# The low half of a split state on VectorE in two pieces, the first gather taken apart among the up products, and the expert ids written first

## The chip, the core and the metric

The kernel runs on one NeuronCore of a Trainium2 chip. TensorE (PE in the rows, PEld for its weight loads), VectorE (DVE), ScalarE (ACT) and GpSimd (POOL) compute; SyncE (SP) issues the DMAs that bring the weights from HBM. The metric is the device time of one execution in microseconds. Three runs of the kernel before gave a median of 1363.94 us.

## What is computed

Two transformer blocks stand behind each other; the second has two layers. Each of the three layers ends in a mixture of experts over 256 tokens of width 1024: 32 experts in 4 groups, of which every token takes two. Cut to the part that the change touches:

```python
logit_g = (h @ w_rg + b_rg).astype(F32)
grp = jnp.argmax(logit_g, axis=-1)
logit_e = (h @ w_re + b_re).astype(F32).reshape(n_tok, N_GROUPS, EXPERTS_PER_GROUP)
logit_e = jnp.take_along_axis(logit_e, grp[:, None, None], axis=1)[:, 0]
top_v, top_i = lax.top_k(logit_e, TOP_K)
gate = jax.nn.softmax(top_v, axis=-1) * p_grp
...
def expert_block(args):
    xb, e = args
    g, u = jnp.split(xb @ w_up[e], 2, axis=-1)
    return (jax.nn.silu(g) * u) @ w_down[e]
```

The state `h` is the RMS-normed residual stream. The second block's layers do the same with a hidden width of 256 where the first has 512. All data is float32.

## The kernel before

**Stages.** `first_phase` computes the first block's attention and `second_phase` that of a layer of the second block. Each ends in `out_route`, which projects the attention's output, adds it to the residual X, and routes the tokens. `moe_phase` then runs the experts. So there are three boundaries between an attention and its experts, at about 280, 815 and 1147 us of the trace. In the rows they are told apart by these times.

**Weights.** All weights go through one `Stream`: a list of 1 MB pieces in a fixed order, and a ring of 23 SBUF slots. `pump` issues pieces on SP's queue as long as slots are free; `release` gives a slot back and pumps. SP works its queue strictly in order: an issue whose slot is still read by somebody holds up all that stand behind it. It also waits until the DMA eight places before it has landed, so at most eight are in flight. The experts of a layer come in blocks `p`. The first two blocks are static: their experts are known when the program is built, and their 24 pieces can be issued before the routing is done. From the third block on the experts are those that the routing ranks highest. Their pieces are in the stream as functions: `pump` stops at them until `publish` has filed the routing under its key, and then SP loads each expert's number from the tile `info` (lines 429 and 446) before it issues.

**The router in two token halves.** In `out_route` a token half `a` has 128 tokens. `choose(a)` is a chain of 18 small VectorE operations (lines 689 to 706) that ends in the mask `mk`. `place(a)` counts with TensorE (lines 715 and 717) each token's place in its expert, and VectorE writes `rpm` (line 718). `split(a)` takes the normed state apart into a high half `xh` (ScalarE, line 721) and a low half `xl`, the rounding rest, which the float32r matmuls need both of. For `a == 0` VectorE computes `xl` in one operation over 1024 columns (line 723). For `a == 1` ScalarE writes the normed state into a spare tile (line 726) and GpSimd subtracts (line 727). After it the slots `spent[1]` and `X.u` are released, in that order.

**The first experts.** In `moe_phase`, `sel_p(0)` builds the selection matrix P from `rpm` (line 1488). `gather(0, dp)` for dp = 0 to 3 fills two of the eight column blocks of `xg` each: 8 matmuls `xh`, `xl` by P into one PSUM bank (line 1520), one copy out by ScalarE (line 1528) and one by VectorE (line 1530 or 1532). `up(p)` multiplies `xg` with the up weights, column block by column block `dt` = 0 to 7 (line 1704); after every second `dt` in the first block's layer, after every fourth in the second block's, it releases the slots that it has used. For p = 0 it calls `hooks` between the column blocks: `rank_experts` (after dt 1), `place_units` and `gates` (after dt 3), `publish` (after dt 5), `unit_gates` (after dt 7). `publish` computes the ids (line 1614) and two further tables (lines 1617 to 1620) on TensorE, and then VectorE writes `info` (line 1621). `mm()` hands out PSUM banks in turn: two in the first block's layer, three in the second block's.

**Order.** The schedule is manual: each engine works its instructions in the order in which the program calls them. The tiles' readers and writers give the waits.

Of the kernel before, what the change touches and what calls it, by code (L numbers as in the profile page):

```python
# [10 lines left out]
F32 = mybir.dt.float32  # L11
F32R = mybir.dt.float32r
I32 = mybir.dt.int32
AF = mybir.ActivationFunctionType
# [358 lines left out]
def hybrid_kernel(ctx: ExitStack, tc: tile.TileContext, A, out, dbg=None):  # L373
# [115 lines left out]
    def cmc(n):  # L489
        return cm[:, CM[n][0]:CM[n][1]]  # L490
# [112 lines left out]
    def out_route(kind, O, E, finish, wr, brow, xT, tmp, spent):  # L603
# [31 lines left out]
        def group(a, c0, n, j):  # L635
            po = R.mm()[:, 0:n]
            sl = slice(c0, c0 + n)
            out_mm(O, po, a, sl, range(8))
            finished(po, a, sl, j)
# [29 lines left out]
        def scored(a):  # L669
            dve.scalar_tensor_tensor(R.L[:, a], pls[a][:, 0:36], rr[a], brow, op0=OP.mult, op1=OP.add)  # L670
# [39 lines left out]
        def place(a):  # L710
            mkf = R.mk.rearrange("p a g e -> p a (g e)")
            if a == 0:
                R.pr = R.mm()
            o = R.pr[:, 32 * a:32 * a + 32]
            pe.matmul(o, lhsT=cmc("strict"), rhs=mkf[:, a], start=True, stop=(a == 0), skip_group_check=True)
            if a == 1:
                pe.matmul(o, lhsT=ones, rhs=mkf[:, 0], start=False, stop=True, skip_group_check=True)
            dve.scalar_tensor_tensor(R.rpm[:, a], o, 1.0, mkf[:, a], op0=OP.add, op1=OP.mult)

        def split(a):  # L720
            act.activation(xh[:, a], X.t[:, a], AF.Copy, scale=rr[a])
            if a == 0:
                dve.scalar_tensor_tensor(xl[:, a], X.t[:, a], rr[a], xh[:, a].bitcast(F32), op0=OP.mult, op1=OP.subtract)
            else:
                t = tmp[:, 0:1024]
                act.activation(t, X.t[:, a], AF.Copy, scale=rr[a])
                pool.tensor_sub(xl[:, a], t, xh[:, a].bitcast(F32))

        group(0, 512, 512, 1)
        trans(0, 0, 4, True)  # L730
# [5 lines left out]
        scored(0)  # L736
        choose(0)
        split(0)
        group(1, 512, 256, 3)
        trans(1, 0, 4, False)  # L740
        group(1, 768, 256, 4)
# [5 lines left out]
        root(1)  # L747
        logits(1, range(4, 8))
        scored(1)
        choose(1)  # L750
        place(0)
        for j in range(4):
            start_y(j)
        place(1)
        split(1)
        S.release(*spent[1], X.u)
        R.xh, R.xl = xh, xl
        return R

# [682 lines left out]
    def moe_phase(kind, l, R, final=None):  # L1442
# [7 lines left out]
        with ExitStack() as es:  # L1450
# [81 lines left out]
                        dve.tensor_scalar(xg[:, dt], o, s, None, op0=OP.mult)  # L1532

            sel_p(0)
            cn = wx.tile([32, 1], F32, name="cn")
            dve.tensor_copy(cn, pr[0:32, 64:65])
            for dp in range(4):
                gather(0, dp)
            mark("moe")

            th = wx.tile([32, 4], F32, name="th")
# [70 lines left out]
            def publish():  # L1612
                pq = mm()
                pe.matmul(pq[0:1, 0:NS], lhsT=cmc("eid")[0:32], rhs=ind, start=True, stop=True)
                for a in range(2):
                    o = pq[:, 64 + a * NS:64 + (a + 1) * NS]
                    pe.matmul(o, lhsT=R.rT[:, a * 128:(a + 1) * 128], rhs=ind, start=True, stop=False,
                              skip_group_check=True)
                    pe.matmul(o[:, NR:], lhsT=ones[0:32], rhs=base, start=False, stop=True, skip_group_check=True)
                    pe.transpose(pq[0:32, 256 + a * 128:384 + a * 128], R.Gd[:, a], ident)  # L1620
                dve.tensor_copy(R.info[:, 0:NS], pq[0:1, 0:NS])
                R.rp = wx.tile([128, 2, NS], F32, name="rp")
                dve.tensor_copy(R.rp.rearrange("p a u -> p (a u)"), pq[:, 64:64 + 2 * NS])
                R.regs = {}
                routes[key] = R
                S.pump()
                R.gT = wk.tile([32, 256], F32, name="yl")
                act.activation(R.gT, pq[0:32, 256:512], AF.Copy)

# [15 lines left out]
            class Ring:  # L1645
# [21 lines left out]
                def up(self, p, dt, hf):  # L1667
                    if dt % per == 0 and hf == 0:
                        self.us = self.units(p, ("up", dt), blocks[p].n)
                    return [u.t.rearrange("p (k c) -> p k c", k=per)[:, dt % per, hf * 512:(hf + 1) * 512]  # L1670
                            for u in self.us]
# [34 lines left out]
            def up(p, src, hooks=()):  # L1706
                c = (p % 2) * 128
                pu = R.up()
                xg = grp[p // 2][2]
                hooks = dict(hooks)  # L1710
                for dt in range(8):
                    for hf in range(nh):
                        pair_mm(pu[:, hf * 512:(hf + 1) * 512], lambda a, b: xg[:, dt, c + a:c + b], src.up(p, dt, hf),
                                dt == 0, dt == 7)
                    src.up_done(p, dt)
                    for h in hooks.get(dt, ()):
                        h()
                hd = wk.tile([128, hid], F32, name="hd")
                act.activation(hd, pu[:, 0:hid], AF.Silu)  # L1719
                dve.tensor_mul(hd, hd, pu[:, hid:uw])  # L1720
                st[p] = K()
                st[p].hd = hd
# [100 lines left out]
                    act.preload_act_table_set("natural_log_exp_and_others")  # L1823
                    spare(p + 1, nun)

            count_hooks = {1: [rank_experts], 3: [place_units, gates], 5: [publish], 7: [unit_gates]}
            ring_src = Ring(S)
            ng = (NL + 1) // 2
            ALL = [(0, 0), (1, 0), (0, 1), (1, 1)]
            for p in range(NL + 1):  # L1830
                g = p // 2
                if p == NL - 2:
                    nun = nc.values_load(R.info[0:1, NS:NS + 1], engines=[ENG.PE, ENG.Activation, ENG.DVE, ENG.Pool],
                                         min_val=0, max_val=SPARE)
                if p == NL - 1:
                    S.reserve(5 if final == 1 else 6)
                if p == NL:
                    scat(p - 2, ALL[2:])
                    down(p - 1, ring_src)
                    break  # L1840
                if p > 0 and p % 2 == 0 and g + 1 < ng:
                    sel_p(g + 1)
                if p == 0:
                    up(p, ring_src, count_hooks)
                    sel_p(1)
                    sel_g(0)
                else:
                    up(p, ring_src)
                for z in range(2):
                    if p % 2 == 1 and g + 1 < ng:  # L1850
                        for dp in (2 * z, 2 * z + 1):
                            gather(g + 1, dp)
                    if p >= 2 and z == 0:
                        scat(p - 2, ALL[2:])
                if p % 2 == 1 and g + 1 < ng:
                    sel_g(g + 1)
                if p == NL - 1:
                    act.preload_act_table_set("natural_log_exp_and_others")
                    spare(NL, nun)
                if p > 0:  # L1860
                    down(p - 1, ring_src)
                tr(p)
# [428 lines left out]
```

## Time and profile before

| | |
|---|---|
| median of 3 runs (lowest to highest) | 1363.94 us (1363.77 to 1364.64) |
| the profiled execution: its own time, its span | 1363.06 us, 1361.4 us |
| busy share of the span: PE, PEld, DVE, ACT, POOL | 89%, 48%, 31%, 25%, 7% |
| weight queue: share of the 16 DMA engines, data | 82.2%, 458.04 MB |
| chain that ended last: PE, DMA, DVE, ACT | 54%, 33%, 6%, 4% |
| granted TensorE clock, mean | 0.96 |

The busy shares are averages over stages that differ: in some the PE sets the pace, in others the DMA queue has no gap. The chain of waits tells which, stretch by stretch. A granted clock of 1.00 is 2.4 GHz and 0.50 is 1.2 GHz. A row of a timeline gives start, duration, engine, line, operation and tiles, and in brackets the idle time before it.

### The profile page before, as it was taken

To read this page: it belongs to the slowest core of one execution; us is meant where nothing else is said; L and a number is where in the kernel's file an instruction comes from. 1 tells how busy PE (TensorE), PEld (TensorE's weight loads), DVE (VectorE), ACT (ScalarE), POOL (GpSimd) and SP (SyncE) were. 2 spreads that over 40 slices of the span, in tenths; PEclk is the share of its full clock that TensorE was granted. 3 is DMA by queue.
4 is the path that set the end of the run, shared out by engine and by line. 5 is a ranking of instruction groups with operands and counts; after the bars stand their busy time and mean duration, and the time that the engine had idled before them with its cause. 6 is when DMAs were issued, how large, how long until landed. Compare 5 with 4: busy or idle time off the path is not lost.

```text
span 1361.4 us, 18797 instructions
## 1 busy us (share of the span) xinstructions
PE 1205.6 (89%) x7310; PEld 652.9 (48%) x7310; DVE 424.1 (31%) x1001; ACT 338.6 (25%) x696; POOL 93.9 (7%) x79
## 2 busy tenths in 40 slices
PE   5999999999977799999679998998778999999775
PEld 3788765554221154443158655443217756444211
DVE  5456453352101021221155444221005535322102
ACT  4432343221000010110146522211015642212102
POOL 1344100000000000000012100000000210000000
PEclk9999999999988899999889999999889999999998
DMA  9645517959999999999994548999999365899995
GB/s 370 256 178 186 201 32 321 389 217 394 421 421 421 422 421 420 422 420 421 420 419 180 220 191 341 420 421 421 421 418 403 124 278 216 362 421 421 421 421 227
DMA packets 64540, 459.45 MB, mean 337 GB/s; under 512 B 7408, under 2 KB 7728, under 8 KB 9904
## 3 DMA queue, kind: packets, MB, share of 16 engines
q1 hardware_dynamic: 64432, 458.04, 82.2%
q8 instruction: 65, 1.06, 0.3%
q14 instruction: 43, 0.35, 0.1%
HBM read 466.40 MB, written 1.05 MB: 343 GB/s over the span
## 4 chain that ended last, share of the span: by engine, by line
PE 54%; DMA 33%; DVE 6%; ACT 4%; issue 2%; POOL 0%; SPq 0%; ACTq 0%; DVEq 0%; POOLq 0%
DMA ring<-in_dn_dram 14%; PE up L1704 12%; PE ps L561 10%; DMA ring<-in_gu_dram 10%; DMA ring<-in_up_dram 9%; PE mm L1704 6%; PE mm L596 5%; PE mm L1520 3%; PE ps L2001 3%; PE tr L596 2%; PE po L1770 1%; PE ps L957 1%; PE tr L1770 1%; PE ps L1972 1%; PE po L2125 1%
## 5 line engine op out<-in xcount | busy, mean ns | idle before, releaser
L1704 PE MATMUL up<-ring,xg 128*32 128x512 f32 (+2 forms) x2016 | 368.0, 632 | 55.1 <-DMA ring<-in_gu_dram 31.5
L1704 PEld LDWEIGHTS up<-ring,xg 128*32 128x32 f32 (+2 forms) x2016 | 103.9, 126 | 288.5 <-issue 184.8
L1704 PE MATMUL mm<-ring,hdT 128*32 128x512 f32 (+2 forms) x1008 | 192.7, 633 | 29.9 <-DMA ring<-in_dn_dram 18.3
L561 PE MATMUL ps<-ring,ring 128*128 128x256 f32 (+1 forms) x960 | 144.5, 308 | 1.4 <-POOL ring L896 0.6
L561 PEld LDWEIGHTS ps<-ring,ring 128*128 128x128 f32 x960 | 129.2, 192 | 20.9 <-issue 4.8
L1720 DVE TENSOR_TENSOR hd<-hd,up 128x256 f32<-128x256 f32 (+1 forms) x32 | 16.7, 520 | 358.0 <-ACT hd L1719 339.5
L1704 PEld LDWEIGHTS mm<-ring,hdT 128*32 128x32 f32 (+2 forms) x1008 | 52.4, 125 | 143.3 <-issue 97.9
L1719 ACT ACTIVATE hd<-up 128x256 f32<-128x256 f32 (+1 forms) x32 | 14.9, 465 | 369.3 <-PE up L1704 369.3
L1520 PEld LDWEIGHTS mm<-P,ring 128*128 128x128 f32 x512 | 66.6, 200 | 12.4 <-issue 9.0
L1520 PE MATMUL mm<-P,ring 128*128 128x256 f32 x512 | 70.6, 295 | 0.6 <-DVE xg L1530 0.3
L596 PE MATMUL mm<-ring,ring 128*128 128x512 f32 (+1 forms) x192 | 64.1, 487 | 0.0
L1746 DVE SCALAR_TENSOR_TENSOR yl<-mm,gt,yh 128x512 fp32r<-128x512 f32 x38 | 28.5, 751 | 110.3 <-ACT yh L1745 110.3
L1745 ACT ACTIVATE yh<-mm,gt 128x512 fp32r<-128x512 f32 x38 | 26.1, 687 | 105.2 <-PE mm L1704 70.2
L1741 DVE SCALAR_TENSOR_TENSOR mm<-mm,gt,gmod 128x512 f32<-128x512 f32 x24 | 18.2, 758 | 106.7 <-PE mm L1704 106.7
L1742 ACT ACTIVATE yh<-mm 128x512 fp32r<-128x512 f32 x23 | 13.7, 597 | 141.2 <-DVE mm L1741 141.2
L2001 PE MATMUL ps<-ring,ring 128*128 128x256 f32 x384 | 48.6, 286 | 0.0
L2001 PEld LDWEIGHTS ps<-ring,ring 128*128 128x128 f32 x384 | 46.9, 192 | 0.7 <-ACT ring L1977 0.4
L596 PEld LDWEIGHTS mm<-ring,ring 128*128 128x128 f32 x192 | 35.8, 190 | 23.7 <-issue 21.5
L1984 POOL TENSOR_SCALAR ring<-ring,fr 128x1024 f32<-128x1024 f32 x2 | 6.7, 3370 | 421.2 <-DMA ring<-in_win_dram 421.2
L822 POOL TENSOR_TENSOR ring<-ring,ring 128x1024 fp32r<-128x1024 f32 x12 | 29.9, 2492 | 58.0 <-ACT ring L821 50.9
L1954 DVE TENSOR_TENSOR ring<-ring,ring 128x1024 fp32r<-128x1024 f32 x24 | 29.0, 1255 | 13.3 <-ACT ring L1950 13.3
L1770 PE MATMUL po<-yh,sm 128*128 128x512 f32 x61 | 30.6, 502 | 1.7 <-ACT yh L1742 1.0
(460 smaller groups left out, 1336.9 us busy)
## 6 DMA issues: line engine op xcount, KB each, us to landing
ring<-in_gu_dram SPq DMA_DIRECT2D x128, 1024.0 KB, 19.7
ring<-in_dn_dram SPq DMA_DIRECT2D x124, 1024.0 KB, 19.7
ring<-in_up_dram SPq DMA_DIRECT2D x120, 1024.0 KB, 19.5
ring<-in_wmod_dram SPq DMA_DIRECT2D x24, 1024.0 KB, 6.9
ring<-in_win_dram SPq DMA_DIRECT2D x24, 1024.0 KB, 11.4
ring<-in_wout_dram SPq DMA_DIRECT2D x12, 1024.0 KB, 18.4
ring<-in_c_dram SPq DMA_DIRECT2D x2, 896.0 KB, 13.7
ring<-in_wsm_dram SPq DMA_DIRECT2D x2, 784.0 KB, 14.9
```

Source lines behind the costliest of these rows:

```text
L561: pe.matmul(out, lhsT=a, rhs=b, start=first and i == 0, stop=last and i == 2, skip_group_check=True)
L596: pe.matmul(po, lhsT=O.mixT[:, s, a * 128:(a + 1) * 128], rhs=O.w[2 * c + s // 4][:, s % 4, sl.start - 512 * c:sl.stop - 512 * c], start=( ...
L822: (pool if q else dve).tensor_sub(lo[:, sl], u.t[:, sl], hi[:, sl].bitcast(F32))
L1520: pe.matmul(o, lhsT=xx[:, a, dt * 128:(dt + 1) * 128], rhs=P[:, a], start=(k == 0), stop=(k == 3))
L1704: pe.matmul(out[w * e:w * e + w], lhsT=x_of(w * e, w * e + w), rhs=wt, start=start, stop=stop)
L1720: dve.tensor_mul(hd, hd, pu[:, hid:uw])
L1741: dve.scalar_tensor_tensor(pd, pd, s.gt, gmod[:, hf * 512:(hf + 1) * 512], op0=OP.mult, op1=OP.mult)
L1745: act.activation(yh, pd, AF.Copy, scale=s.gt)
L1746: dve.scalar_tensor_tensor(yl, pd, s.gt, yh.bitcast(F32), op0=OP.mult, op1=OP.subtract)
L1770: pe.matmul(y[2 * a + hf], lhsT=s.sm[:, a * 128:(a + 1) * 128], rhs=s.y[hf][i], start=False, stop=True, skip_group_check=True)
L1954: dve.tensor_sub(lo[:, sl], u.t[:, sl], hi[:, sl])
L2001: pe.matmul(p[:, f * 256:(f + 1) * 256], lhsT=w[pw][:, dt, f * 128:(f + 1) * 128], rhs=hT[ph][:, dt], start=(i == 0 and f == 0 and dt == 0 ...
```

## The change

It has four parts. The function names are those of the section above; line numbers in the rows of the changed program are some lines higher.

- `split(1)` loses its second ScalarE pass and the GpSimd subtraction and is called before `choose(1)`. VectorE computes `xl` of the second token half as it does for the first, by a new `split_low`, in two pieces of 512 columns: one between the two `place` calls, the other in `R.rest()`, which `moe_phase` calls after `sel_p(0)`.
- The release of `spent[1]` and `X.u` moves with the second piece into `R.rest()`.
- The four parts of the first gather become hooks. Parts 0 and 1 stand before the up products, with `rank_experts` between them. Parts 2 and 3 stand between the up products.
- `publish` computes the ids alone, files the routing and pumps. The two tables that it also made move into `tables`, called after `gates`. `place_units` and `publish` come earlier: after dt 0 and dt 1 in the first block's layer, after dt 1 and dt 3 in the second block's.

```diff
         def split(a):
             act.activation(xh[:, a], X.t[:, a], AF.Copy, scale=rr[a])
-            if a == 0:
-                dve.scalar_tensor_tensor(xl[:, a], X.t[:, a], rr[a], xh[:, a].bitcast(F32), op0=OP.mult, op1=OP.subtract)
-            else:
-                t = tmp[:, 0:1024]
-                act.activation(t, X.t[:, a], AF.Copy, scale=rr[a])
-                pool.tensor_sub(xl[:, a], t, xh[:, a].bitcast(F32))
+
+        def split_low(a, c0, c1):
+            dve.scalar_tensor_tensor(xl[:, a, c0:c1], X.t[:, a, c0:c1], rr[a], xh[:, a, c0:c1].bitcast(F32), op0=OP.mult,
+                                     op1=OP.subtract)
...
+        split(1)
         choose(1)
         place(0)
+        split_low(1, 0, 512)
         for j in range(4):
             start_y(j)
         place(1)
-        split(1)
-        S.release(*spent[1], X.u)
+
+        def rest():
+            split_low(1, 512, 1024)
+            S.release(*spent[1], X.u)
+        R.rest = rest
...
             sel_p(0)
+            R.rest()
             cn = wx.tile([32, 1], F32, name="cn")
             dve.tensor_copy(cn, pr[0:32, 64:65])
-            for dp in range(4):
-                gather(0, dp)
...
             def publish():
                 pq = mm()
                 pe.matmul(pq[0:1, 0:NS], lhsT=cmc("eid")[0:32], rhs=ind, start=True, stop=True)
+                dve.tensor_copy(R.info[:, 0:NS], pq[0:1, 0:NS])
+                R.regs = {}
+                routes[key] = R
+                S.pump()
+
+            def tables():
+                pq = mm()
                 for a in range(2):
...
-            count_hooks = {1: [rank_experts], 3: [place_units, gates], 5: [publish], 7: [unit_gates]}
+            first = [lambda dp=dp: gather(0, dp) for dp in range(4)]
+            if kind == 1:
+                first_hooks = {-1: [first[0], rank_experts, first[1]], 0: [place_units], 1: [publish, first[2]],
+                               3: [gates, first[3]], 5: [tables], 7: [unit_gates]}
+            else:
+                first_hooks = {-1: [first[0], rank_experts, first[1]], 1: [place_units], 3: [publish, first[2]],
+                               4: [gates, first[3]], 6: [tables], 7: [unit_gates]}
```

VectorE at the first boundary, before, from the last operation of `choose(1)` (`mk`) to the key of the ranking (`kd`); `xg` is the gathered state:

```order
L706 TENSOR_TENSOR mk<-o_2071,o_2072 128x32 [waits DVE_49]
L718 SCALAR_TENSOR_TENSOR rpm<-mm,mk 128x32 [waits PE_49]
L718 SCALAR_TENSOR_TENSOR rpm<-mm,mk 128x32 [waits DVE_49,PE_49]
L1460 COPY bias_2264<-modT 128x8
L1488 TENSOR_TENSOR P<-cm,rpm 128x256 [waits DVE_49] x2
L1536 COPY cn<-mm 32x1 [waits PE_49]
L1530 TENSOR_SCALAR xg<-mm,G_88,bias_2264 128x256 [waits Activation_49] x4
L1548 TENSOR_SCALAR key_2322<-cn,cm 32x1 [waits DVE_49]
L1549 TENSOR_SCALAR kd<-cm,key_2322 32x32 [waits DVE_49]
```

VectorE at the same place of the changed kernel; `ring_2063` is `xl`, `ring_77` is X:

```order
L706 TENSOR_TENSOR mk<-o_2071,o_2072 128x32 [waits DVE_49]
L718 SCALAR_TENSOR_TENSOR rpm<-mm,mk 128x32 [waits PE_49]
L724 SCALAR_TENSOR_TENSOR ring_2063<-ring_77,r_2206,ring_2062 128x512 [waits Activation_49]
L718 SCALAR_TENSOR_TENSOR rpm<-mm,mk 128x32 [waits DVE_49,PE_49]
L1464 COPY bias_2261<-modT 128x8
L1492 TENSOR_TENSOR P<-cm,rpm 128x256 [waits DVE_49] x2
L724 SCALAR_TENSOR_TENSOR ring_2063<-ring_77,r_2206,ring_2062 128x512
L1541 COPY cn<-mm 32x1 [waits PE_49]
L1551 TENSOR_SCALAR key_2278<-cn,cm 32x1 [waits DVE_49]
L1552 TENSOR_SCALAR kd<-cm,key_2278 32x32 [waits DVE_49]
L1534 TENSOR_SCALAR xg<-mm,G_88,bias_2261 128x256 [waits Activation_49]
L1560 TENSOR_SCALAR cmp<-mm,key_2278 32x32 [waits PE_49]
```

The two pieces of the low half stand where VectorE had nothing of the kind; the key of the ranking now comes before the first copy out of the gather and no longer after all four.

TensorE at the first boundary, before, from the gather's first matmul to the ids (`ring_2062` is `xh`, `ring_2063` is `xl`; the four parts stand in one block):

```order
L1520 MATMUL mm<-P,ring_2062 128x256 [waits DVE_49,PE_49,Activation_49]
L1520 MATMUL mm<-P,ring_2063 128x256
...
L1704 MATMUL up<-ring_1799,xg 64x512 [waits DMAHW4_49]
...
L1553 MATMUL mm<-kd,ones 32x32 [waits DVE_49,Activation_49]
L1704 MATMUL up<-ring_120,xg 64x512 [waits DMAHW6_49]
...
L1569 MATMUL mm<-nu,cm 32x1 [waits DVE_49,Activation_49]
L1704 MATMUL up<-ring_74,xg 64x512 [waits DMAHW0_49]
...
L1614 MATMUL mm<-ind,cm 1x42 [waits DVE_49]
```

And of the changed kernel:

```order
L1524 MATMUL mm<-P,ring_2062 128x256 [waits DVE_49,PE_49,Activation_49]
...
L1556 MATMUL mm<-kd,ones 32x32 [waits DVE_49,PE_49]
L1524 MATMUL mm<-P,ring_2062 128x256 [waits DVE_49]
...
L1710 MATMUL up<-ring_1799,xg 64x512 [waits DMAHW4_49]
...
L1572 MATMUL mm<-nu,cm 32x1 [waits DVE_49]
...
L1617 MATMUL mm<-ind,cm 1x42 [waits DVE_49,Activation_49]
L1524 MATMUL mm<-P,ring_2062 128x256 [waits Activation_49]
...
L1710 MATMUL up<-ring_120,xg 64x512 [waits DMAHW6_49]
```

The ranking's matmul stands between the gather's parts 0 and 1, the ids come after the first two column blocks (`ring_1799`) and not after six, and part 1 of the gather waits for VectorE, which copies part 0 out of the bank.

## Rows read from the trace of the kernel before

**Rows 1.** Chain of waits, two of its pieces: start us, us, what
```profile
338.66 11.77 DMA ring<-in_up_dram
1319.40 17.39 DMA ring<-in_dn_dram
```
**Rows 2.** Busy time by stretch: us, engines (instructions), TensorE clock, DMA share, GB/s
```profile
268.00:310.00 42.00, 38.40 (x213) 23.73 (x213) 22.71 (x98) 9.01 (x19) 2.34 (x1) 0.96 0.55 208
310.00:686.00 376.00, 330.82 (x1801) 127.03 (x1801) 57.53 (x107) 38.26 (x66) 0.00 (x0) 0.95 1.01 421
824.60:830.70 6.10, 5.98 (x58) 2.05 (x60) 3.70 (x18) 1.07 (x3) 0.00 (x0) 1.00 0.17 34
832.00:1020.00 188.00, 165.58 (x1056) 65.61 (x1055) 33.10 (x79) 29.59 (x57) 0.00 (x0) 0.95 1.01 420
1155.60:1161.70 6.10, 5.98 (x55) 2.12 (x58) 3.55 (x18) 1.24 (x3) 0.00 (x0) 1.00 0.12 17
1162.00:1337.00 175.00, 151.89 (x1028) 62.06 (x1024) 32.21 (x83) 28.25 (x56) 0.00 (x0) 0.97 1.01 420
```
**Rows 3.** Timeline at the end of choose(1), first and third boundary
```profile
281.03 0.19 DVE L702 TENSOR_TENSOR o<-l,m 128x32 f32<-128x32 f32 x1
281.20 2.34 POOL L727 TENSOR_TENSOR ring<-ring,ring 128x1024 fp32r<-128x1024 f32 x1 [48.61 <-ACT ring L726]
281.26 2.33 DVE L703 TENSOR_TENSOR o<-o,rg 128x32 f32<-128x32 f32 x1
...
1146.65 2.37 DVE L703 TENSOR_TENSOR o<-o,rg 128x32 f32<-128x32 f32 x1
```
**Rows 4.** Chain of waits, the PE pieces around the first up products and two gathers
```profile
285.83 5.66 PE mm L1520 x32
...
298.83 0.15 PE mm L1569 x2
...
299.36 3.58 PE up L1704 x16
...
491.75 1.91 PE mm L1520 x16
...
819.96 5.26 PE mm L1520 x32
```
**Rows 5.** Timeline and busy time by stretch: VectorE and ScalarE operations of these steps
```profile
271.17 1.28 DVE L723 SCALAR_TENSOR_TENSOR ring<-ring,r,ring 128x1024 fp32r<-128x1024 f32 x1
290.57 0.57 ACT L1528 ACTIVATE xg<-mm,bias,G 128x256 f32<-128x256 f32 x1 [1.14 <-PE mm L1520]
291.17 0.54 DVE L1530 TENSOR_SCALAR xg<-mm,G,bias 128x256 f32<-128x256 f32 x1 [1.17 <-ACT xg L1528]
...
295.29:297.14 1.85, 1.85 (x10) 0.66 (x12) 1.61 (x9) 0.00 (x0) 0.00 (x0) 1.00 0.34 89
```
**Rows 6.** Timeline: the ids, and SP's issues (start of the first, us to the last)
```profile
295.10 4.08 SPq L332 DMA_DIRECT2D ring<-in_dn_dram  x3
304.65 0.19 DVE L1621 CAST info<-mm 1x42 int32<-1x42 f32 x1 [1.62 <-PE mm L1620]
306.73 8.47 SPq L332 DMA_DIRECT2D ring<-in_up_dram  x7
829.10 1.28 SPq L332 DMA_DIRECT2D ring<-in_dn_dram  x3
```
**Rows 7.** Issues on SP at 295.1 and at 335.7: time to landing
```profile
DMA to landing us min/median/max: 4.8/4.8/4.8
DMA to landing us min/median/max: 9.7/9.7/9.7
```
**Rows 8.** Busy time by stretch: an idle TensorE, the clock after it, a shorter idle
```profile
281.95:284.42 2.47, 0.00 (x1) 0.00 (x1) 2.31 (x5) 0.00 (x0) 1.59 (x1) 1.00 0.01 3
286.99:290.40 3.41, 3.41 (x19) 3.41 (x18) 1.09 (x2) 1.13 (x2) 0.00 (x0) 0.50 0.91 384
832.00:835.00 3.00, 2.16 (x18) 1.23 (x21) 1.65 (x10) 0.31 (x1) 0.00 (x0) 1.00 1.02 423
```

More of the change, by code (lines that the diff above doesn't have):

```diff
@@ L738, in out_route @@
         split(0)
+        split_low(0, 0, 1024)
         group(1, 512, 256, 3)
@@ L1620, in publish @@
                     pe.transpose(pq[0:32, 256 + a * 128:384 + a * 128], R.Gd[:, a], ident)
-                dve.tensor_copy(R.info[:, 0:NS], pq[0:1, 0:NS])
                 R.rp = wx.tile([128, 2, NS], F32, name="rp")
                 dve.tensor_copy(R.rp.rearrange("p a u -> p (a u)"), pq[:, 64:64 + 2 * NS])
-                R.regs = {}
-                routes[key] = R
-                S.pump()
                 R.gT = wk.tile([32, 256], F32, name="yl")
@@ L1710, in up @@
                 hooks = dict(hooks)
+                for h in hooks.get(-1, ()):
+                    h()
                 for dt in range(8):
@@ L1843, in moe_phase @@
                 if p == 0:
-                    up(p, ring_src, count_hooks)
+                    up(p, ring_src, first_hooks)
                     sel_p(1)
```

## The prediction

> **What bounds the kernel now.** I read three views in this order. First the chain of waits: in each of the three expert stages it ends in pieces of DMA, the first from 338.66 us on, the last from 1319.40 us [rows 1]. So the end of an expert stage is the landing of its last weights. Then the busy time by stretch: from 310 to 686, 832 to 1020 and 1162 to 1337 us the DMA engines are busy all the time, at 420 to 421 GB/s [rows 2]. A stream without gaps can't be made faster, it can only begin earlier. So the third question is what stood still before it. From 268 to 310 us the DMA engines are busy 0.55 of 42 us, that is, 18.9 us are lost; at the other two boundaries a gap of 6.1 us precedes the stream, with 0.17 and 0.12 [rows 2]. The timelines show what ends these gaps. At the first boundary SP issues three pieces from 295.10 us on, as up products give slots back, then waits for the ids, which VectorE writes at 304.65, and issues the first ranked expert at 306.73 us [rows 6]. At the other two SP waits for slots alone: it issues three more static pieces from 829.10 us on, when the first four column blocks are through [rows 6]. What comes earlier on this path, choose, gather, up products, ids, is worth its time in full; what comes earlier after the stream has begun is worth nothing. The attention behind each stage starts when the stage ends, so gains of the three boundaries add up.
>
> **The subtraction leaves GpSimd.** While GpSimd's 2.34 us run, VectorE's L703 takes 2.33 us, where its neighbour L702, of the same kind and size, takes 0.19; at the third boundary it takes 2.37 [rows 3]. Without GpSimd the operation should take 0.19 like its neighbour: 2.14 us at each boundary. In exchange VectorE does two pieces of 512 columns. The same operation over 1024 columns took 1.28 us [rows 5], so a piece takes 0.64 at the least and, with a fixed part, some 0.7. The first stands where VectorE waits for place(1)'s matmuls anyway; it costs about nothing. The second stands behind P and puts off the ranking's key by 0.7 us; TensorE has part 0 of the gather (1 us) as cover, and what is left is counted below. ScalarE's removed pass was off the path. The release of X.u now waits for the second piece, about 284.6 us instead of GpSimd's end at 283.54 [rows 3]; the slot before it in SP's queue, which GpSimd held, is free some 7 us earlier. Together these move two pieces within a gap that stays open, and I count nothing.
>
> The Trainium skill (Perfetto Trace Analysis, Optimizing Scalar/DVE Operations) says that work may be worth taking off a saturated VectorE, which speaks against moving it there. By that rule, with both pieces on the path, each boundary would lose 1.3 us more, and the sum below would come to 1351.4 us. Here VectorE is busy 22.71 of 42 us at the first boundary [rows 2]: not saturated, though on the path. The rule is weak here.
>
> **First boundary.** Times are those of the trace, the new ones worked out. The gather starts at 285.83 us [rows 4]; 2.14 earlier is 283.69. A part of the gather is 8 matmuls: 16 take 1.91 us at 2.4 GHz, so 0.96 [rows 4]. Part 0 ends at 284.65. Part 1 now waits until both copies out are done, since this layer's PSUM banks are two: 0.57 on ScalarE, 0.54 on VectorE [rows 5], and some 0.1 to hand over. It starts at 285.87 and ends at 286.83; the key and the ranking's matmul fit in the wait. Two column blocks take 3.58 us [rows 4], so one takes 1.79: dt 0 ends at 288.62. place_units' matmuls stand there: from 298.83 to 299.36 they took 0.53 [rows 4]. They need the ranking's nine VectorE operations, 1.85 us [rows 5], which start behind the copy at about 285.8 and end at 287.7: no wait. dt 1 ends at 290.94, and two slots come back then; before it was 295.10 [rows 6]. The ids (0.2), part 2 of the gather (0.96) and dt 2 and 3 (3.58) end at 295.7, where before the third static piece left at about 298.9. The ids are long there; SP needs 1.9 us from the ids to the first ranked issue, as 304.65 plus 0.19 to 306.73 [rows 6] shows. So the first ranked piece is issued at about 297.7 and not 306.73: 9.0 us earlier. Its data can follow the static pieces without a gap.
>
> Then the slots bound it. The tables took publish's matmuls from 302.94 to about 304.6, 1.5 without the ids [rows 4, 6]. With part 3 (0.96) and four more column blocks (7.16) the last column block ends at 305.3; before it was 304.6 plus 3.58, 308.2. TensorE is thus 2.9 us ahead from there on, and an issue that waits for a slot of the next blocks comes 2.9 us earlier. The tightest such issue stood at 335.7 us and landed 9.7 us later, while an issue with nothing ahead of it takes 4.8 [rows 7]. It can be 9.7 minus 4.8, 4.9 us, plus 2.9 earlier: 7.8 us. That is less than 9.0, and I take **7.8 us**. Its bounds are 2.9 (only what TensorE gains) and 9.0.
>
> **Second and third boundary.** Here slots decide. Up to the release: before, four parts (5.26 us [rows 4], part of it at the low clock) and the ranking's matmul of 0.2; now two parts (1.91), the ranking, and place_units (0.53), which now stands ahead. There are three banks, so part 1 doesn't wait for copies, but the ranking waits for its key: P, the second piece, three small operations, 2.1 us from the start of P; part 0 ends after 1.5. That is 0.6. So 5.26 minus 1.91, 0.53 and 0.6 is 2.2, and with 2.14 from GpSimd **4.3 us**. The gap is 6.1 us long [rows 2], more can't come. The ids, now right behind the release, come in time for the fourth slot, since three static pieces fill 7.5 us. Bounds: 2.14 and 6.1.
>
> **The sum.** 7.8 + 4.3 + 4.3 = 16.4 us. The profiled execution took 1363.06 us, with a span of 1361.4; its own sum is 1346.7. The median of the runs is 0.9 higher, 1363.94: **1347.5 us**. Edits at nothing: gates and tables later (the tables are needed for the second gather, behind the whole first up, and TensorE no longer waits for the gates in front of them); POOL's queue loses an entry that nobody else stood behind.
>
> **The clock.** From 281.95 to 284.42 TensorE was idle 2.47 us, and from 286.99 to 290.40 its granted clock was 0.50, 1.2 GHz [rows 8], over the gather. My terms have 2.4 GHz. The change leaves smaller holes: about 0.9 us around place(1), then the wait for copies (1.2) or for the key (0.6). A stretch of 3 us with 0.84 idle kept 1.00 [rows 8]; the new holes together are larger than that one, in some 4 us, but spread. I hold it likelier than not that the clock stays in most places. Where it falls, 3.41 us at half speed cost 1.7 us on the path.
>
> The Trainium skill (TensorE: Matmul & The Clock Gate, What's actually happening) says that activity releases the low clock, and that where the change falls varies from run to run for one kernel. So runs may differ by a place; one trace can't show that.
>
> **Rivals.**
> 1. The clock falls at all three boundaries in the new holes. For it: float32r parts of 1 us and tiny matmuls are little work for 4 us. Against: the holes are short. 1347.5 + 3 x 1.7 = 1352.6 us.
> 2. The ids come earlier, but at the first boundary the stream gains only TensorE's 2.9 us, since slots and not ids hold it throughout. For it: SP waits for slots in every one of these stretches. Against: nine microseconds of the gap are behind the ids alone. 1347.5 + 4.9 = 1352.4 us.
> 3. Only GpSimd's stall comes back, and the new waits eat what taking the gather apart gives: 3 x 2.14 = 6.4, so 1357.5 us.
> 4. Slower: the low clock, which covers one stretch of 3.41 us now, extends into the first up products, because the gather's pieces no longer keep TensorE busy. Up to the release these take 7.16 us at the first boundary; at 1.2 GHz they cost as much again, and with parts 0 and 1 some 9 us. It decides from 4.3 us on, at all three places; at 5.3 each it would end at 1367 us. Against: the up products stand without holes once started, and the clock came back after 3.41 us with TensorE busy.
> 5. It does nothing: the ends of the stages are set by slots further on. 1364 us. Against: the streams have no gaps to swallow a gain [rows 2].
>
> **How the numbers follow.** Forecast 0.52, rival 1 0.18, rival 2 0.13, rival 3 0.08, rival 4 0.04, rival 5 0.05. The likeliest is the sum, and a place with low clock moves it by 1.7; I give 1348 us. The range leaves out rivals 3 to 5 (0.17) and takes in rivals 1 and 2, with the upper bounds of the terms (9.0 and some of 6.1) below: 1344 to 1355. A run of this kernel can tell 0.2%, 2.7 us, from no change. Faster by more: 0.91; within: 0.05; slower: 0.04.
>
> **What would show it.** In the changed profile L703 should take 0.19 everywhere; TensorE should be idle under 1 us before place(1); the ids should be written near 291.3 and the first ranked issue near 298 us; the gaps ahead of the second and third stream should shrink from 6.1 to about 2 us, and the streams should run at 1.01 as before. Wrong would be the forecast if a stream shows new gaps after its start, if the clock rows show 0.50 over the up products, or if part 1 of the gather starts later than 1.3 us after part 0.

## The result, and the profile after

The changed kernel took 1350.14 us (median of 4 runs, 1348.00 to 1355.35), the kernel before 1364.29 beside it. The ratio is 0.9895, with a 95% interval of 0.9859 to 0.9930. The time lies in the forecast range, 2.1 us above the forecast itself. The profiled execution took 1348.00 us, its span is 1346.0.

Busy time by stretch, after; the columns are those of [rows 2]:

```profile
268.00:310.00 42.00, 39.53 (x217) 23.08 (x217) 21.79 (x96) 8.36 (x18) 0.00 (x0) 0.97 0.72 268
310.00:681.00 371.00, 326.39 (x1794) 125.98 (x1790) 56.69 (x103) 37.68 (x65) 0.00 (x0) 0.95 1.01 419
330.30:348.37 18.07, 18.07 (x136) 5.86 (x134) 3.97 (x9) 1.68 (x3) 0.00 (x0) 1.00 0.99 398
335.00:337.00 2.00, 2.00 (x10) 0.84 (x8) 0.00 (x0) 0.00 (x0) 0.00 (x0) 1.00 0.90 270
818.70:824.80 6.10, 5.54 (x50) 2.65 (x42) 3.20 (x17) 1.26 (x4) 0.00 (x0) 1.00 0.75 261
830.41:833.82 3.41, 3.41 (x20) 0.87 (x16) 0.35 (x1) 0.22 (x1) 0.00 (x0) 0.50 1.00 416
1145.90:1152.00 6.10, 5.54 (x46) 2.65 (x42) 3.33 (x18) 1.26 (x4) 0.00 (x0) 1.00 0.72 262
```

The stretch ahead of the first stream moves 268 GB/s where it moved 208 [rows 2]. Stretches of 6.1 us around the later gaps now carry data for 0.75 and 0.72 of the time, where it was 0.17 and 0.12. The stream runs at 1.01 as before, but for a new thin place at 335 to 337 us, with 270 GB/s. The low clock at the second boundary now falls at 830.41, behind the gather, when the stream is already running.

Timeline, after, at the first boundary (SP's rows: start of the first issue, us to the last):

```profile
281.58 0.19 DVE L703 TENSOR_TENSOR o<-o,rg 128x32 f32<-128x32 f32 x1
282.60 0.41 PE L715 MATMUL mm<-mk,cm 128*128 128x32 f32 x2 [0.33 <-DVE rpm L718]
285.01 12.25 SPq L332 DMA_DIRECT2D ring<-in_dn_dram  x4
292.21 0.19 DVE L1618 CAST info<-mm 1x42 int32<-1x42 f32 x1 [0.72 <-PE mm L1617]
299.16 8.68 SPq L332 DMA_DIRECT2D ring<-in_up_dram  x5
```

L703 is back at 0.19 us, and TensorE waits 0.33 us for place(1) where it waited 2.47. The ids are written at 292.21, and the first ranked issue leaves at 299.16 and not at 306.73 [rows 6].

Chain of waits, after (start us, us, what):

```profile
284.01 1.31 PE mm L1524 x8
286.54 1.21 PE mm L1524 x8
287.75 1.87 PE up L1710 x8
...
292.18 1.15 PE mm L1524 x8
...
663.39 17.76 DMA ring<-in_dn_dram
...
1323.43 3.62 PE mm L1710 x26
```

The first stage's last DMA lands at 663.39 + 17.76 = 681.15 us. The gather's parts start 2.53 us apart, since part 1 waits for both copies.

Timeline at the second boundary, the first matmul of place(0) before and after, and the issues of the three static pieces that the up products release, after (before they began at 829.10 [rows 6]):

```profile
812.24 0.39 PE L715 MATMUL mm<-mk,cm 128*128 128x32 f32 x2
806.76 0.39 PE L715 MATMUL mm<-mk,cm 128*128 128x32 f32 x2
819.40 1.58 SPq L332 DMA_DIRECT2D ring<-in_dn_dram  x3
```

So the release comes 12.6 us behind place(0), where it came 16.9 behind it.

To compare runs free of what the clock does in the attention, I take for each boundary the time from the first matmul of place(0) to the landing of one late piece of weights, the same piece in every kernel (in the first two stages the last one of the chain). Before, these are 407.9, 208.3 and 196.1 us. The table gives how much shorter they are in each profile. Median and ratio are of all executions of a kernel, against executions of the kernel before that ran beside it (1363.23 to 1371.48 us in the 17 beside e9 to e12); the stages are of one profiled execution each, so the two need not agree to the us. A star marks a boundary where the granted clock fell to 0.50 within the gather's parts, in a kernel in which VectorE does the subtraction.

| kernel | 1st | 2nd | 3rd | sum | median, us | ratio to before (95%) |
|---|---|---|---|---|---|---|
| the change | 5.1 | 3.8 | 4.3 | 13.3 | 1350.14 | 0.9895 (0.9859 to 0.9930) |
| the change again (e12) | 2.5* | 4.1 | 2.7* | 9.3 | 1351.69 | 0.9879 (0.9857 to 0.9902) |
| split only (e1) | 2.5 | 3.0 | 2.1 | 7.6 | 1354.10 | 0.9912 (0.9895 to 0.9930) |
| gather only (e2) | -3.2 | -1.1 | -1.9 | -6.2 | 1371.95 | 1.0046 (1.0032 to 1.0059) |
| ids only (e3) | 3.0 | -3.4 | -3.0 | -3.4 | 1365.65 | 1.0005 (0.9994 to 1.0016) |
| no split (e4) | -0.2 | -0.8 | 0.0 | -1.0 | 1363.39 | 0.9983 (0.9970 to 0.9996) |
| ids late (e5) | 1.6 | 2.8 | 2.0 | 6.4 | 1358.08 | 0.9958 (0.9940 to 0.9975) |
| gather whole (e6) | 5.9 | 1.8 | 1.8 | 9.5 | 1354.06 | 0.9923 (0.9900 to 0.9947) |
| delay in the change (e7) | 3.8 | 2.1* | 4.4 | 10.2 | 1353.07 | 0.9910 (0.9893 to 0.9926) |
| delay before (e8) | -0.2 | -0.2 | -1.4 | -1.8 | 1364.93 | 1.0004 (0.9990 to 1.0018) |
| down first (e9) | 5.6 | 4.1 | 2.7* | 12.4 | 1350.76 | 0.9881 (0.9856 to 0.9906) |
| filled hole (e10) | -0.7 | -0.6 | -0.3 | -1.6 | 1363.79 | 0.9984 (0.9970 to 0.9997) |
| two edits more (e11) | 6.6 | 2.5* | 4.3 | 13.4 | 1348.67 | 0.9880 (0.9856 to 0.9904) |

Where the code of a boundary is the same and its clock stayed, profiles agree within 0.3 us (3.8, 4.1, 4.1 at the second; 4.3, 4.4, 4.3 at the third). Where GpSimd subtracts, the low clock can last longer than in the profile of before: the third stage of e8, whose code there is that of before, is 1.4 us longer.

### The profile page after: what moved, and what is told of

It reads as the page before. It is cut to its first block, busy times and chain, and to the rows that moved or that the text cites. A ratio compares the mean times of both kernels' runs of the same rounds, so it can differ in the third digit from the quotient of the medians.

```text
span 1346.0 us, 18786 instructions
## 1 busy us (share of the span) xinstructions
PE 1201.5 (89%) x7310; PEld 650.3 (48%) x7310; DVE 421.9 (31%) x1007; ACT 335.8 (25%) x693; POOL 86.9 (6%) x76
## 4 chain that ended last, share of the span: by engine, by line
PE 52%; DMA 36%; ACT 5%; DVE 5%; issue 2%; SPq 0%; POOL 0%; ACTq 0%; DVEq 0%; POOLq 0%
DMA ring<-in_dn_dram 14%; DMA ring<-in_gu_dram 13%; PE up L1710 11%; PE ps L561 10%; DMA ring<-in_up_dram 8%; PE mm L1710 5%; PE mm L596 5%; PE ps L2015 3%; PE mm L1524 2%; PE tr L596 2%; PE ps L961 1%; PE po L1778 1%; PE ps L1986 1%; PE tr L1778 1%; ACT ring L1964 1%
## 5 line engine op out<-in xcount | busy, mean ns | idle before, releaser
L1710 PE MATMUL mm<-ring,hdT 128*32 128x512 f32 (+2 forms) x1008 | 190.0, 624 | 30.1 <-DMA ring<-in_dn_dram 18.2
L1524 PEld LDWEIGHTS mm<-P,ring 128*128 128x128 f32 x512 | 63.2, 188 | 16.3 <-issue 11.9
L1968 DVE TENSOR_TENSOR ring<-ring,ring 128x1024 fp32r<-128x1024 f32 x24 | 29.0, 1255 | 13.3 <-ACT ring L1964 13.3
```

The lines of the kernel that those rows point to most:

```text
L1524: pe.matmul(o, lhsT=xx[:, a, dt * 128:(dt + 1) * 128], rhs=P[:, a], start=(k == 0), stop=(k == 3))
L1710: pe.matmul(out[w * e:w * e + w], lhsT=x_of(w * e, w * e + w), rhs=wt, start=start, stop=stop)
L1968: dve.tensor_sub(lo[:, sl], u.t[:, sl], hi[:, sl])
```

## The experiments

**Theories.** A: the stall on GpSimd and the low clock behind it are most of the gain, and at the first boundary slots bind once the ids are early. B: taking the gather apart, with the early ids, is most of it. C: the first boundary is bound by TensorE alone. D: the start of the stream or the ids bind there, not slots further on.

### e1: the split alone

```diff
 (the change, with the gather and the ids as before)
+            for dp in range(4):
+                gather(0, dp)
...
+                first_hooks = {1: [rank_experts], 3: [place_units, gates], 5: [publish], 7: [unit_gates]}
```

> Stage lengths are taken from the last group of the output projection ahead of the routing to the TensorE piece behind the stage's last DMA: 413.88, 214.08 and 199.10 us in the kernel before; the change shortens them by 5.1, 3.8 and 4.1 us. Only the split moves to VectorE; gather in one block, ids with the tables, both where they stood. Theory A (the stall and the low clock that follows it are most of the gain): the gather starts 2.1 us earlier and runs at 2.4 GHz, 1.7 us more; everything behind it, ids and slots, comes 3.8 us earlier, so each stage is 3 to 3.8 us shorter, 10 us in all. Theory B (taking the gather apart and the early ids are most of it): only the stall comes back, 2.1 us at each, 6.4 in all; the clock still falls over the gather.

Its stages are 2.5, 3.0 and 2.1 us shorter, between the two theories in the sum, and the clock does what A says. Timeline of e1, second boundary, and its busy time by stretch there:

```profile
823.96 1.28 SPq L332 DMA_DIRECT2D ring<-in_dn_dram  x3
815.96 4.11 PE L1524 MATMUL mm<-P,ring 128*128 128x256 f32 x32
```

```profile
815.00:823.00 8.00, 7.59 (x69) 5.17 (x72) 4.84 (x16) 1.90 (x4) 0.00 (x0) 1.00 0.91 380
```

The gather takes 4.11 us at 1.00, where it took 5.26 [rows 4]. Counted from place(0), which begins at 810.41 in e1, the gather starts 2.17 us earlier, and the three static pieces behind the release are issued 3.3 us earlier (the first 13.5 us behind place(0) against 16.9): 2.17 for the stall and 1.15 for the clock. A had the clock too dear, with 1.7. What the slots gain isn't all kept. The first ranked issue comes 3.1 us earlier too at the third boundary, and the stage is 2.1 us shorter; where the rest goes isn't settled.

### e2: the gather apart alone

```diff
 (GpSimd subtracts, ids and tables in one)
+                first_hooks = {-1: [first[0], rank_experts, first[1]], 1: [first[2]], 3: [place_units, gates, first[3]],
+                               5: [publish], 7: [unit_gates]}
```

> Only the gather is taken apart (ranking between its parts 0 and 1); GpSimd subtracts, ids with the tables. Theory A: TensorE still idles 2.5 us, the clock falls, and at the second and third boundary the slots come back 1 to 1.5 us earlier, at the first the ids stay late, 0 to 0.5; 2 to 3.5 us in all. Theory B: 2 us or more at each of the later boundaries, over 4 in all.

Both theories fall: the kernel is slower, by 0.46%. Busy time by stretch of e2, first boundary, and its timeline there:

```profile
285.08:295.32 10.24, 8.55 (x34) 5.92 (x36) 4.26 (x20) 1.13 (x2) 0.00 (x0) 0.50 0.51 205
```

```profile
290.50 2.08 PE L1522 MATMUL mm<-P,ring 128*128 128x256 f32 x8 [0.99 <-DVE xg L1532]
292.51 5.03 PE L1704 MATMUL up<-ring,xg 128*64 128x512 f32 x16
```

TensorE still idles 2.48 us, and the clock falls, not for 3.41 us as before [rows 8] but for 10.24. Within it the parts take 2.1 us each, TensorE waits for copies in between, and the first two column blocks take 5.03 us, where they took 3.58 [rows 4]. This is the mechanism of the prediction's fourth rival, the low clock that reaches into the up products. Here it follows the idle time that the split takes away; e12 shows it, shorter, without that idle time.

### e3: the ids alone

```diff
 (GpSimd subtracts, gather in one block)
+                first_hooks = {0: [rank_experts], 1: [place_units], 2: [publish], 3: [gates], 5: [tables], 7: [unit_gates]}
+            else:
+                first_hooks = {1: [rank_experts], 2: [place_units], 3: [publish], 4: [gates], 6: [tables], 7: [unit_gates]}
```

> Only the ids come alone and early (after dt 2 in the first block's layer, dt 3 in the second block's), gather in one block, GpSimd subtracts. Theory A: at the first boundary the first ranked issue comes 5 to 6 us earlier than 306.73, and the stage is 3 us shorter, where the slots of 335.7 bind (9.7 us to landing against 6.5 in the changed kernel); at the other two nothing or 0.5 us lost, since place_units stands ahead of the release. Theory C (first boundary bound by TensorE alone, rival 2 of the prediction): 0 at the first as well.

The first stage is 3.0 us shorter, as A says and against C (the first ranked issue leaves at 302.07, 4.7 us earlier and not 5 to 6): TensorE is not ahead there (the issue that stood at 335.7 comes 0.6 us later, counted from place(0)), and yet the stream gains. The later stages lose 3.4 and 3.0 us, which neither had. Timeline of e3, second boundary:

```profile
816.75 6.26 PE L1522 MATMUL mm<-P,ring 128*128 128x256 f32 x32
...
827.01 0.19 PE L1571 MATMUL mm<-nu,cm 32*32 32x1 f32 x2 [0.98 <-DVE nu L1567]
```

The low clock covers the gather for longer (6.26 us against 5.26), and place_units, one hook behind the ranking, makes TensorE wait 0.98 us ahead of the release.

### e4: the change without the split

```diff
 (the change, with the old second half of the state)
-            split_low(1, 512, 1024)
+        act.activation(t, X.t[:, 1], AF.Copy, scale=rr[1])
+        pool.tensor_sub(xl[:, 1], t, xh[:, 1].bitcast(F32))
```

> The change without its first part: GpSimd subtracts and holds L703. Theory A: the stages are 1.5 to 3 (first), 1.3 and 1.3 us shorter than before, since stall and low clock stay; some 5 us in all instead of 13. Theory B: 3 us at the first and 2 at each of the others, 7 or more.

Less than either theory had: -0.2, -0.8 and 0.0 us, 0.17% in the time. Two parts of three give next to nothing without the first. Busy time by stretch of e4, second boundary:

```profile
820.12:826.95 6.83, 6.77 (x34) 4.62 (x38) 3.54 (x16) 0.95 (x2) 0.00 (x0) 0.50 0.70 289
```

The clock is low for 6.83 us, over both parts and the first up products.

### e5: the change with late ids

```diff
-                               3: [gates, first[3]], 5: [tables], 7: [unit_gates]}
+                first_hooks = {-1: [first[0], rank_experts, first[1]], 0: [place_units], 1: [first[2]], 3: [gates, first[3]],
+                               5: [publish], 7: [unit_gates]}
 (publish with the tables again; dt 6 in the second block's layers)
```

> The change with the ids left beside the tables (after dt 5 and dt 6). Theory A: the first stage keeps 1 to 1.5 of its 5.1 us, since the ids come at about 303.5 and hold the ranked pieces; the other two stages keep all (3.8 and 4.1), as the three static pieces cover the ids. Theory C (first boundary bound by TensorE alone): the first stage keeps 4 or more.

The first stage keeps 1.6 of its 5.1 us, just above A's 1 to 1.5; C falls. But the later stages lose as well, 1.0 and 2.3 us, where A had nothing. SP's rows of e5, first and second boundary:

```profile
304.99 8.47 SPq L332 DMA_DIRECT2D ring<-in_up_dram  x7
830.88 9.40 SPq L332 DMA_DIRECT2D ring<-in_gu_dram  x8
```

At the second boundary the first ranked issue comes 21.2 us behind place(0), in the change 15.2, while the third static piece lands at 22.9: an issue that stands 1.7 us ahead of the end of the stream is too late. So the early ids are needed at all three boundaries once the slots come back early.

### e6: the change with the gather in one block

```diff
+            for dp in range(4):
+                gather(0, dp)
...
+                first_hooks = {0: [rank_experts], 1: [place_units], 2: [publish], 3: [gates], 5: [tables], 7: [unit_gates]}
+            else:
+                first_hooks = {1: [rank_experts], 2: [place_units], 3: [publish], 4: [gates], 6: [tables], 7: [unit_gates]}
```

> The change with the gather in one block again: ranking after dt 0, place_units after dt 1, ids after dt 2 in the first block's layer; after dt 1, 2, 3 in the second block's. Theory A: at the first boundary the parts cost TensorE waits (1.2 us for the copies) that the block does not have, and its slots bind further on, so the first stage is shorter than in the change, by 6 to 6.7 us against before; the later stages are 0.5 us longer than in the change, 3.3 each. Theory B: the first stage loses 1 us or more against the change, and the later two 1.5 to 2 each.

At the first boundary A is right but for 0.1 us (5.9; its lower end was 6): the block is 0.8 us better than the parts, and the thin place at 335 to 337 us is gone. At the later two B is right: 1.8 us each, 2.0 and 2.6 less than the change. Busy time by stretch of e6, first boundary, and its timeline, second boundary:

```profile
335.00:337.00 2.00, 2.00 (x20) 0.81 (x20) 0.76 (x1) 0.58 (x2) 0.00 (x0) 1.00 1.02 422
```

```profile
819.14 0.19 PE L1574 MATMUL mm<-nu,cm 32*32 32x1 f32 x2 [0.98 <-DVE nu L1570]
```

The whole gather stands ahead of the release, and then TensorE waits 0.98 us for the ranking: the release comes 15.2 us behind place(0) and not 12.6. Of these 2.6 us the block itself is 0.9 (13.5 in e1, with the block, against 12.6 in e5, with the parts). The rest is the ranking and place_units, which the early ids put ahead of the release; whether a block could have early ids without that wait was not tried.

### e7 and e8: more work on TensorE behind the first up products

```diff
+            def delay():
+                for _ in range(2):
+                    p = mm()
 (8 gather matmuls into p, read by nobody)
...
-                               3: [gates, first[3]], 5: [tables], 7: [unit_gates]}
+                               3: [gates, first[3]], 5: [tables], 7: [unit_gates, delay]}
```

> The change with 16 gather matmuls more, 1.9 us at 2.4 GHz, on TensorE behind the first up products of the first block's layer alone; their result is not used. Theory A (slots that TensorE gives back at 334 us bind the first stage): the stage is 1.9 us longer, all of it. Theory D (the ids or the start of the stream bind): 0 to 0.5 us longer.

> The same 16 matmuls in the kernel before, at the same place. Theory A: the issue of 335.7 us has 9.7 us to landing, 3 more than needed, so the stage is 0 to 0.3 us longer. Theory D': slots bound the stage before as well, 1.9 us longer.

The 16 matmuls take 2.18 us in the one and 2.17 in the other, 0.7 of it in a hole that TensorE had anyway; the issues behind come 1.5 us later. In the change the stage becomes 1.4 us longer (A had 1.9, all of the delay; 1.4 is nearly all of the 1.5 that reached the issues), in the kernel before 0.2. So slots bind the changed first stage, and didn't bind the one before, as A says of both. Busy time by stretch of e7:

```profile
335.00:337.00 2.00, 2.00 (x12) 0.73 (x8) 0.52 (x1) 0.00 (x0) 0.00 (x0) 1.00 0.60 119
```

The thin place of the change, 270 GB/s, has become a gap with 119.

### e9: the first down products ahead of the second gather

```diff
+                early = kind == 1 and p == 1
+                if early:
+                    down(0, ring_src)
...
-                if p > 0:
+                if p > 0 and not early:
                     down(p - 1, ring_src)
```

> The change with the down products of the first expert block ahead of the second gather, in the first block's layer alone. Measured from the first matmul of place(0) to the landing of the stage's last weights, the first stage took 407.9 us before and 402.8 in the change. Theory A (slots that TensorE gives back late leave the stream short of work): the slots of 334.2 us come back some 5 us earlier, the gap of about 0.9 us at 335 to 337 us closes, and the first stage is 0.8 to 1.5 us shorter than in the change. Theory D (the start of the stream alone binds): under 0.3 us.

Busy time by stretch of e9, the same stretch behind place(0) as 330.30 to 348.37 in the change, and the thin place:

```profile
331.00:349.06 18.06, 15.68 (x160) 7.69 (x160) 4.67 (x12) 3.35 (x6) 0.00 (x0) 1.00 1.01 420
335.00:337.00 2.00, 1.72 (x15) 1.51 (x14) 0.58 (x2) 1.13 (x2) 0.00 (x0) 1.00 1.03 430
```

The stretch ahead of it, in the change and in e9:

```profile
291.87:330.30 38.43, 36.78 (x238) 17.47 (x238) 8.42 (x30) 7.15 (x13) 0.00 (x0) 1.00 0.97 383
292.56:331.00 38.44, 37.89 (x200) 15.39 (x200) 7.63 (x27) 5.49 (x10) 0.00 (x0) 1.00 0.97 380
```

The thin place is closed, 420 GB/s against 398 over the stretch, worth 0.9 us of stream. The stage is 0.5 us shorter, between A's 0.8 and D's 0.3. Some 0.3 of the rest went ahead of it, where e9 moved 380 GB/s and the change 383.

### e10: the hole filled in the kernel before

```diff
             start_y(j)
+        for _ in range(5):
+            pe.matmul(R.y[3], lhsT=ident, rhs=X.t[:, 1, 512:1024], start=True, stop=False, skip_group_check=True)
         place(1)
```

> The kernel before with five more matmuls of 0.47 us on TensorE, in the 2.47 us in which it waits for place(1) at each boundary; they write the same values again. The stall stays. Theory A (the low clock over the gather comes from that idle time): the clock is 1.00 over the gather, which takes 4.1 us and not 5.2 to 5.7, and the later two stages are 1.1 to 1.5 us shorter, the first 1 to 1.5. Theory B (the clock falls there for another reason): 0.50 stays in the rows, no stage is shorter by more than 0.3 us.

Timeline of e10, second boundary, and its busy time by stretch there:

```profile
816.92 4.46 PE L755 MATMUL tr<-ring,cm 128*128 128x512 f32 x10
822.45 4.11 PE L1522 MATMUL mm<-P,ring 128*128 128x256 f32 x32
```

```profile
816.00:830.00 14.00, 13.59 (x87) 7.75 (x85) 7.74 (x25) 2.17 (x5) 2.35 (x1) 1.00 0.68 273
```

Each call of this kind is two instructions, so the filling took 4.46 us and not 2.35, and place(1) comes 1.65 us later; the stages are no shorter. But the clock stays at 1.00 at all three boundaries, beside the same GpSimd operation (2.35 us of it in the row), and the gather takes 4.11 us and not 5.26. The release, for a start 1.55 us later, comes 0.4 later. So the idle time, and not the operation beside it, causes the low clock there, and the clock costs 1.15 us on this path. The filling is longer than the hole; a shorter one was not tried.

### e11 and e12: two edits more, and the change once more

e11 has, in the first block's layer alone, the gather of e6 and the order of e9; the other layers are those of the change.

> The change with two edits in the first block's layer alone: the gather in one block (ranking after dt 0, place_units after dt 1, ids after dt 2), and the down products of the first expert block ahead of the second gather. Theory A: the first stage is 7 to 7.5 us shorter than before (5.9 with the gather in one block, and the gap of 1.4 us at 335 to 337 us closed), the later two 3.8 and 4.3 as in the change: 2 us faster than the change. Theory D: 5.9 and no more at the first, 0.8 us faster than the change.

> The changed kernel once more, beside the others. If the clock alone makes its runs differ, its stages are 5.1, 3.8 and 4.3 us shorter than before where the clock stays at 1.00 over the gather, and some 1.5 to 1.8 us less at a place where it falls, as at the second boundary of the run with the delay.

e11's first stage is 6.6 us shorter than before, between A's 7 and D's 5.9, and its median 1348.67 us, but its ratio, 0.9880, can't be told from that of e12, 0.9879. The expectation's gap of 1.4 us at 335 to 337 us was that of e7, read for e6's; e6 has none there, and so there was little for the second edit to close. Chain of waits of e12, its first up products at the first boundary; busy time by stretch of e12, first and third boundary, and of e11, second:

```profile
288.09 2.59 PE up L1710 x8
286.11:289.52 3.41, 3.41 (x12) 2.22 (x14) 1.93 (x10) 0.56 (x1) 0.00 (x0) 0.50 0.68 286
1142.86:1146.27 3.41, 3.41 (x18) 2.33 (x22) 2.48 (x11) 0.83 (x2) 0.00 (x0) 0.50 1.00 418
```

```profile
813.77:817.18 3.41, 3.41 (x16) 1.89 (x20) 2.48 (x11) 0.52 (x2) 0.00 (x0) 0.50 1.01 416
```

The same program that kept its clock at all three boundaries in one execution lost it at two in another, and those stages are 2.6 and 1.7 us longer, where the expectation had 1.5 to 1.8. At the first boundary the low clock reaches into the up products: 8 of them take 2.59 us there, and 1.87 in the first profile of the change.

## Why the prediction was right, point by point

**What bounds.** It held: the streams run without large gaps in both kernels, stages end in DMA, and what comes earlier at the boundary comes earlier at the end. Two of the prediction's signs of being wrong did show in a small way: a thin place behind the start of the first stream (270 GB/s at 335 to 337 us), and in one of the change's two profiles 0.50 over the first up products (e12).

**GpSimd.** It held: L703 at 0.19, place(1) 2.14 to 2.18 us earlier behind place(0), against 2.14. The slots that wait for the second half of the state gave nothing, as counted: at the third boundary their first issue leaves 5.3 us earlier, and the second lands 12.7 us behind place(0) and not 13.1, so what they carry ends hardly earlier. The Trainium skill (SBUF — State Buffer, SBUF: two separate sides) says that VectorE and GpSimd share a port pair that one of them holds for a whole instruction; the trace agrees, with 2.33 us beside GpSimd's 2.34 and 0.19 without.

**First boundary.** The mechanism held: the early ids move the bound to slots further on (e5, e7, e8), and rivals 2 and 5 fall (e3: 3.0 us without any lead of TensorE). The size was off, 5.1 us and not 7.8. The lead of TensorE, taken as 2.9 us, was 1.8, counted from place(0) as the 5.1 are (the issue of 335.67 left at 334.21, and place(0) began 0.3 us later). A part of the gather costs 1.15 to 1.31 us by itself and not half of the 1.91 that 16 matmuls in a row cost, 0.96. And an issue can't come 4.9 us closer to its landing without loss: this one landed 6.6 us after it left, and the stream was already thin there. 9.7 minus 6.6 plus 1.8 is 4.9, near the 5.1.

**Second and third boundary.** The size held: 3.8 and 4.3 us for 4.3, and the release comes 4.2 us earlier (12.6 against 16.9 us behind place(0)). The split into causes did not. The prediction gave 2.14 to GpSimd and 2.2 to the gather, whose 5.26 us have 1.15 of low clock in them. The split alone brings the release 3.3 us forward, since the clock stays (e1), and the gather's parts on top of it 0.9 (e5); and without the early ids, which the prediction had as merely in time, 1.0 and 2.3 us of the stage are lost again (e5). Rival 3, in which only the 2.14 come back, falls with the release. The three parts don't add: alone they give 7.6, -6.2 and -3.4 us, together 13.3.

**The clock.** The forecast that it stays in most places, and costs 1.7 us where it falls, held in the main. Of the 14 boundaries profiled with the gather apart and early ids on VectorE's subtraction, 5 lost it, at 1.3 to 2.6 us (third: 4.3 to 2.7; second: 3.8 or 4.1 to 2.1 or 2.5; first: 5.1 to 2.5). Of 13 without the 2.5 us of idle time and with other orders (e1, e5, e6, e10, the first of e11) none did. Rival 1 is thus what happens in part in some runs, and a reason why runs of the change differ by some us: the two profiled ones, at 1348.00 and 1352.17 us, lost none and two. What makes one execution lose it and another not stays open. Rival 4 had the same mechanism at all three places; its 7.16 us up to the release are four column blocks, and at the first boundary the release comes after two, 3.58.

**The sum.** The three stages of the profiled run gave 13.3 us, not 16.4. That the total came within 2.1 us owes something to luck: 2.1 of the 15.4 us of span lie outside the stages, where the low clock fell at other times. The chain shows one such place: the last 26 down products took 6.03 us before, from 1336.84 on, and 3.62 after. Chain of waits before, and busy time by stretch before and after:

```profile
1336.84 6.03 PE mm L1704 x26
1336.84:1342.86 6.02, 6.02 (x27) 1.34 (x27) 0.75 (x1) 0.69 (x1) 0.00 (x0) 0.60 0.96 396
1323.43:1327.05 3.62, 3.62 (x27) 0.97 (x27) 0.75 (x1) 0.69 (x1) 0.00 (x0) 1.00 1.02 422
```

The mean granted clock of the same products is 0.60 before and 1.00 after.

## What to carry to other kernels

Before a part of a change is credited, ask what the others do without it: here two of three parts were worth nothing or less until the first took away TensorE's idle time. Work taken apart to fill waits pays per piece, so take it apart only as far as the next release needs; in this kernel it paid where a release comes after four column blocks and cost 0.8 us where one comes after two (e6). A late issue is not late only when its data is missed: with 1 MB pieces, one that left 1.7 us ahead of the end of the stream already cost time.

## What was not expected of the hardware

An idle TensorE of 2.48 us was followed by a low clock at all 15 boundaries profiled where GpSimd subtracts and nothing fills the hole, for 3.41 or 6.83 us with the gather in one block, and for up to 10.24 where small waits followed (e2). And one and the same program, with the same short waits of 0.2 to 0.8 us, kept the clock at a boundary in some executions and lost it in others.
